# Strip-ordered keys, ready-made bias tables and split stack loads in an encoder layer on one core

## The chip, the cores and the metric

The kernel runs on one core of a Trainium2 chip. The metric is device time in microseconds (us). The kernel before took 1975.67 us, the median of 3 runs (1966.2 to 1977.8).

## The reference

One layer of an encoder over 1024 tokens of 1024 features, in float32. A half-weighted SwiGLU feed-forward block, then attention, then a second feed-forward block; each with an RMS norm before and after it.

```python
h = swiglu(rmsnorm(x, ffn1_pre_g[l]), ffn1_w_gate[l], ffn1_w_up[l], ffn1_w_down[l])
x = x + 0.5 * rmsnorm(h, ffn1_post_g[l])
h = rmsnorm(x, mix_pre_g[l])
qkv = (h @ w_qkv[l]).reshape(B, S, 3, N_HEADS, HEAD_DIM).transpose(2, 0, 3, 1, 4)
o_na = neighbourhood_attention(q[:, :N_HEADS_NA], k[:, :N_HEADS_NA], v[:, :N_HEADS_NA], na_rel_bias[l])
o_dil = dilated_mixture_attention(q[:, N_HEADS_NA:], k[:, N_HEADS_NA:], v[:, N_HEADS_NA:], t5_rel_bias)
...
mixed = jnp.concatenate([o_na, o_dil], axis=-1) @ w_out[l]
x = x + rmsnorm(mixed, mix_post_g[l])
h = swiglu(rmsnorm(x, ffn2_pre_g[l]), ffn2_w_gate[l], ffn2_w_up[l], ffn2_w_down[l])
x = x + 0.5 * rmsnorm(h, ffn2_post_g[l])
```

There are 16 heads of 64 features. The eight **neighbourhood** heads see the tokens as a grid of 16 rows by 64 columns: a query attends to 8 rows and 16 columns around it, with a learned bias for each row and column offset, and columns outside its window are masked. The eight **dilated** heads mix attention over three windows (128 neighbours, every fourth token of 512, every sixteenth of 2048), with a bias from 32 buckets of distance; the windows are merged by the denominators of their softmax. The kernel makes the first window in one part and the other two in a second one, in which the tokens are ordered by their residue modulo 4.

## The kernel before

**Stages.** The first feed-forward block, the value projection, the projection to queries and keys (`PairGemm` with the sink `QKPairs`), the four pairs of dilated heads (`DilPair`, pairs 4 to 7), the four pairs of neighbourhood heads (`na_head`, pairs 0 to 3), the output projection and the second feed-forward block follow each other. Each product of large matrices is made from a high and a low part of its operands, in three matrix products (lines 251, 252 and 253).

**Queries and keys.** `QKPairs.put` splits each half of a pair's queries or keys into high and low parts and writes them to DRAM (`c.qk`). The neighbourhood heads cut the grid into eight strips of 8 columns by 16 rows, so 128 tokens. Their queries are written strip by strip; their keys are written in token order, and the score product picks a strip's keys from 16 rows.

**The stack.** For each head `load_stack` brings a tile `st` of 128 partitions by 3 rows of 1024: its upper 64 partitions hold the high part of the queries, the lower 64 the low part; rows 1 and 2 hold the high and the low part of the keys, in both halves. So two matmuls make a score block. Four DMAs load it, all issued by POOL, two for each half of the partitions. The destination has another type (fp32r) than the source. `st` is `q`'s source for the dilated heads: POOL makes a residue-ordered copy of the queries (line 836, `CAST q<-st`), and of the bias table `g` (line 836, `COPY g<-g`).

**A neighbourhood head** takes its strips one by one: two matmuls `sp<-st` (line 1035) give the scores of 128 queries against 2 or 3 strips of keys, DVE adds the bias and takes the maximum (`sb<-sp,nb`, line 847), ACT takes the exponential (line 848), PE transposes the result (`ptp`, line 857), DVE or ACT copies it out of PSUM (`pt`, line 859), and PE multiplies it by the values (`po<-vs,pt`, line 1051). `Ctx.unit` sets PE's order: a strip's scores, then the transposes of the strip three back, then the fillers, then the value product of the strip four back.

**The bias table** `nb` of a head holds 384 columns per query in two forms: as it is for the two strips at the edges, and with the column mask added for the six inner ones. `na_bias` loads the first form from DRAM (`c.nb`) on SP's queue; POOL adds the mask for the second (line 1465, in `next_ready`, called ahead of each head's strip 5 for the head after it).

**Regrouping and merge.** The dilated part of a pair leaves its output in `ob` in another order of tokens. When the pair's second head has finished that part, `regroup` moves it to `obn` with 16 DMAs on SP's queue (line 969); `merge` then weighs the two outputs on DVE and POOL (lines 997, 998) and adds them (line 1001).

**Fillers.** In the last heads, while PE has room, it makes the first sums of the output projection. `nat_fillers` puts 32 closures on a list, each with one step of three matmuls (`nat_mm`) into the PSUM bank `accp`; after four steps ACT copies the bank out (`hs`, line 291). `Ctx.unit` takes them off at an even rate, about one for each strip.

**What sets the order.** PE's order is the program's. A scheduler sets the order of DVE, ACT and POOL's and SP's work from the dependences and from `c.behind`, which holds a step until a named engine's latest instruction has been issued. `c.todo` is a list of small steps that `c.tick` takes one by one. SP and POOL each issue DMAs in their queue's order; an instruction that waits holds all that stands behind it on its engine. `load_head` loads two heads ahead: the stack, the values (`na_v`, 16 DMAs for a pair, line 1009, rows `vs<-v`) and the bias (line 1015).

## Time and profile before

| What | Value |
|---|---|
| Median of 3 runs | 1975.67 us (1966.2 to 1977.8) |
| The profiled execution | 1978.24 us |
| Its span | 1976.5 us |
| Busy time of PE | 1879.0 us (95%) |
| Loads of weights into PE (PEld) | 1565.9 us (79%) |
| DVE, ACT, POOL | 67%, 41%, 16% |

In time from the span's start the stages are: first feed-forward block to about 650, values to 850, queries and keys to 949, dilated heads to 1071, neighbourhood heads to 1225, output projection and second feed-forward block to the end. All that is changed lies between 850 and 1225.

A row of the groups of instructions gives the line, engine and operation, then tile written and tiles read with their shape and type, the number of instructions, busy time and mean ns of one, and the idle time ahead of them with what ended it. In a timeline each row is the start, the duration and the instruction; "SPq" is the time that SP took to issue DMAs; in square brackets stands how long the engine had been idle and what released it. The granted clock is the share of full speed at which PE was let run.

### The profile page before, as it was taken

The numbers are of one execution on the slowest core, as the hardware profiler recorded it, in microseconds if no ns is written. First come the engines' busy times: TensorE is split into PE (matmuls) and PEld (weight loads), VectorE is DVE, ScalarE is ACT, GpSimd is POOL, SyncE is SP. The second block draws the span as 40 slices with busy tenths as digits, with TensorE's granted clock in tenths as the row PEclk, the third lists the DMA queues.
The fourth block names the chain that finished last, engine by engine and source line by source line (L and its number), as shares of the span: only waits on it lengthen the run. The fifth ranks groups of instructions, "written<-read, shape, count | busy, mean of one in ns | idle before, by whom it ended". The sixth has DMA issues, their size and how long they took to land.

```text
span 1976.5 us, 25577 instructions
## 1 busy us (share of the span) xinstructions
PE 1879.0 (95%) x9044; PEld 1565.9 (79%) x9044; DVE 1329.6 (67%) x2235; ACT 808.5 (41%) x1463; POOL 324.2 (16%) x520
## 2 busy tenths in 40 slices
PE   5999999999999999999999788998999999999997
PEld 4888888887888878778898687877888888878886
DVE  5778776775656775577676565676788777745567
ACT  4522233333534454133676545454222333335333
POOL 2101111111000123323434220021011111110000
PEclk8999999999999999999999889999999999999999
DMA  6555565555876667768998962375556655466664
GB/s 232 216 171 176 181 230 203 202 192 213 298 250 207 240 239 261 223 203 245 219 186 153 156 136 48 133 272 203 169 177 206 234 215 192 170 232 221 202 222 141
DMA packets 170433, 398.63 MB, mean 202 GB/s; under 512 B 20080, under 2 KB 41504, under 8 KB 170304
## 3 DMA queue, kind: packets, MB, share of 16 engines
q1 hardware_dynamic: 118800, 222.34, 36.2%
q0 software_dynamic: 50640, 172.55, 27.5%
q10 hardware_dynamic: 864, 2.10, 0.3%
q8 instruction: 71, 1.16, 0.2%
q14 instruction: 58, 0.48, 0.1%
HBM read 272.55 MB, written 127.26 MB: 202 GB/s over the span
## 4 chain that ended last, share of the span: by engine, by line
PE 82%; DMA 7%; DVE 6%; ACT 2%; issue 2%; SPq 1%; POOL 0%; DVEq 0%; POOLq 0%; ACTq 0%
PE mmp L253 17%; PE mmp L252 17%; PE mmp L251 17%; PE accp L252 8%; PE accp L251 8%; PE accp L253 8%; PE trp L159 2%; DMA st<-qk 1%; PE po L1051 1%; PE ptp L857 1%; PE po L951 1%; DMA obn<-ob 1%; DMA praw<-in_wd_dram 1%; PE sp L1035 1%; PE sp L931 1%
## 5 line engine op out<-in xcount | busy, mean ns | idle before, releaser
L251 PE MATMUL mmp<-x,whi 128*128 128x512 f32 (+1 forms) x1464 | 581.0, 397 | 7.5 <-ACT whi L344 3.5
L253 PE MATMUL mmp<-x,wlo 128*128 128x512 f32 (+1 forms) x1464 | 576.7, 394 | 0.7 <-DVE wlo L345 0.6
L252 PE MATMUL mmp<-x,whi 128*128 128x512 f32 (+1 forms) x1464 | 576.1, 394 | 0.5 <-DVE x L161 0.2
L251 PEld LDWEIGHTS mmp<-x,whi 128*128 128x128 f32 x1464 | 278.9, 191 | 67.4 <-ACT whi L344 4.2
L253 PEld LDWEIGHTS mmp<-x,wlo 128*128 128x128 f32 x1464 | 278.7, 190 | 62.4 <-DVE wlo L345 1.9
L252 PEld LDWEIGHTS mmp<-x,whi 128*128 128x128 f32 x1464 | 279.2, 191 | 60.2 <-DVE x L161 1.4
L601 DVE TENSOR_TENSOR pw<-praw,pw 128x1024 fp32r<-128x1024 f32 (+1 forms) x182 | 198.9, 1139 | 127.5 <-ACT pw L600 127.4
L600 ACT CAST pw<-praw 128x1024 fp32r<-128x1024 f32 (+1 forms) x182 | 168.6, 985 | 216.7 <-PE accp L253 168.1
L252 PE MATMUL accp<-pw 128*128 128x512 f32 x616 | 241.5, 392 | 4.9 <-DVE pw L601 4.9
L251 PE MATMUL accp<-pw 128*128 128x512 f32 x616 | 241.8, 393 | 2.5 <-ACT pw L600 2.5
L253 PE MATMUL accp<-pw 128*128 128x512 f32 x616 | 240.9, 391 | 0.0
L344 ACT CAST whi<-wraw 128x1024 fp32r<-128x1024 f32 x129 | 135.3, 1051 | 251.8 <-PE mmp L252 224.1
L345 DVE TENSOR_TENSOR wlo<-wraw,whi 128x1024 fp32r<-128x1024 f32 x129 | 157.7, 1224 | 24.6 <-ACT whi L344 24.5
L252 PEld LDWEIGHTS accp<-pw 128*128 128x128 f32 x616 | 116.3, 189 | 30.4 <-DVE pw L601 6.4
L251 PEld LDWEIGHTS accp<-pw 128*128 128x128 f32 x616 | 116.3, 189 | 27.2 <-ACT pw L600 3.3
L253 PEld LDWEIGHTS accp<-pw 128*128 128x128 f32 x616 | 116.4, 189 | 24.3
L549 POOL DMA_DIRECT2D g<-sg x44 | 23.9, 542 | 473.0 <-DVE sg L542 285.6
L505 DVE TENSOR_TENSOR c<-mmp,u 128x512 f32<-128x512 f32 x52 | 35.9, 691 | 83.5 <-PE mmp L253 83.3
L363 ACT COPY s<-mmp 128x512 f32<-128x512 f32 x52 | 30.5, 587 | 149.4 <-PE mmp L253 147.7
L161 DVE TENSOR_TENSOR x<-trp,x 128x512 fp32r<-128x512 f32 x84 | 57.3, 687 | 36.1 <-ACT x L160 36.0
L344 ACT CAST whi<-traw 128x512 fp32r<-128x512 f32 x52 | 32.4, 622 | 117.3 <-DVE traw L433 58.5
L432 DVE TENSOR_TENSOR wraw<-wraw 128x1024 f32<-128x1024 f32 x52 | 63.6, 1224 | 22.0 <-DMA wraw<-in_wqk_dram 12.6
(223 smaller groups left out, 2767.1 us busy)
## 6 DMA issues: line engine op xcount, KB each, us to landing
praw<-g SPq DMA_DIRECT2D x70, 512.0 KB
wraw<-in_wg_dram SPq DMA_DIRECT2D x44, 512.0 KB
wraw<-in_wu_dram SPq DMA_DIRECT2D x44, 512.0 KB
tr<-in_wd_dram SPq DMA_DIRECT2D x44, 512.0 KB
g<-sg POOLq DMA_DIRECT2D x88, 256.0 KB, 3.7
ts<-tr POOLq DMA_DIRECT2D x22, 1024.0 KB, 4.7
praw<-ts SPq DMA_DIRECT2D x88, 256.0 KB
praw<-in_wd_dram SPq DMA_DIRECT2D x66, 256.0 KB
```

The source lines that it names most:

```text
L159: nc.tensor.transpose(ps[:, j, :], x[:, j * P:(j + 1) * P], c.ident)
L161: nc.vector.tensor_sub(lo, ps, hi.bitcast(F32))
L251: nc.tensor.matmul(out, ahi, bhi, start=start, stop=False, skip_group_check=go_on)
L252: nc.tensor.matmul(out, ahi, blo, start=False, stop=False, skip_group_check=go_on)
L253: nc.tensor.matmul(out, alo, bhi, start=False, stop=stop, skip_group_check=go_on)
L344: nc.scalar.copy(hi, raw)
L345: nc.vector.tensor_sub(lo, raw, hi.bitcast(F32))
L363: self.c.nc.scalar.copy(s, ps)
L432: nc.vector.tensor_sub(r[:, 0:2], r[:, 1:3], r[:, 0:2])
L505: nc.vector.tensor_add(c21, d, u2)
L600: nc.scalar.copy(w[:, side, 0, :m], raw[:, :m])
L601: nc.vector.tensor_sub(w[:, side, 1, :m], raw[:, :m], w[:, side, 0, :m].bitcast(F32))
```

## The change

It has five parts.

1. The keys of the neighbourhood heads are stored by strips, within each of the two halves of the token rows (`p (s r c)`, the halves one after the other), where they were stored in token order. The score product reads them so, and its columns come out strip by strip; the softmax works on contiguous rows.
2. `mask_bias` makes the bias tables of all eight neighbourhood heads during the query and key product: SP loads a table, POOL copies it in the new order of columns and adds the mask for the second form, and POOL's queue writes both to DRAM (`c.nm`). `na_bias` then loads 384 KB in one DMA, and POOL's additions (line 1465) are gone from the heads.
3. The stack's lower half of partitions is loaded by SP's queue, the upper one by POOL's as before; the destination is taken as plain float32.
4. A filler is two steps of three matmuls where it was one, 16 closures instead of 32; `c.rate` follows their number, so that about every second strip has one.
5. `regroup` is called for each quad of blocks (8 DMAs each) instead of once for both. `na_v` loads a pair's values in 8 DMAs of 16 partitions instead of 16 of 8.

The order of PE's and of DVE's work stays but for the fillers. What moves stands on POOL and SP. The first place is POOL in the dilated stage, from the residue-ordered copies to the next pair's stack (`qk_0_83`, `qk_1_84` are the queries and keys of the pair 6, `qk_0_85`, `qk_1_86` those of 7). Before:

```order
L836 COPY q<-st 128x1024
L836 COPY g<-g 128x384
L998 TENSOR_TENSOR oa<-oa,w 128x1024
L997 TENSOR_TENSOR obn<-obn,w 128x8x128
L829 DMA st<-qk_0_83 64x1024
L830 DMA st<-qk_1_84 64x2x1024
L829 DMA st<-qk_0_83 64x1024
L830 DMA st<-qk_1_84 64x2x1024
L836 COPY q<-st 128x1024
```

With the change:

```order
L855 COPY q<-st 128x1024
L1018 TENSOR_TENSOR oa<-oa,w 128x1024
L1017 TENSOR_TENSOR obn<-obn,w 128x8x128
L848 DMA st<-qk_0_83 64x1024
L855 COPY g<-g 128x384
L849 DMA st<-qk_1_84 64x2x1024
L855 COPY q<-st 128x1024
```

The merge's two products stand ahead of the copy of the table, and half of the stack's issues are gone. The second place is SP where the dilated stage ends, from the first value loads of the neighbourhood heads on (`v_87`; `qk_0_71`, `qk_1_72` are the queries and keys of pair 0, `qk_0_73`, `qk_1_74` those of pair 1). Before:

```order
L1009 DMA vs<-v_87 8x8x128 x17
L1015 DMA nb<-nb 128x384
L969 DMA obn<-ob 32x2x132 x16
L1015 DMA nb<-nb 128x384
L1009 DMA vs<-v_87 8x8x128 x15
L1015 DMA nb<-nb 128x384 x2
```

With the change:

```order
L848 DMA st<-qk_0_71 64x1024
L849 DMA st<-qk_1_72 64x2x1024
L1029 DMA vs<-v_87 16x8x128 x8
L1035 DMA nb<-nm 128x768
L989 DMA obn<-ob 32x2x132 x16
L848 DMA st<-qk_0_71 64x1024
L849 DMA st<-qk_1_72 64x2x1024
L1035 DMA nb<-nm 128x768
L848 DMA st<-qk_0_73 64x1024
L849 DMA st<-qk_1_74 64x2x1024
L1029 DMA vs<-v_87 16x8x128 x8
```

The 16 regrouping DMAs are still together, and behind them now stands half of the second head's stack, ahead of its bias table. The third place is POOL at the same point of the program. Before:

```order
L829 DMA st<-qk_0_71 64x1024
L830 DMA st<-qk_1_72 64x2x1024
L1465 TENSOR_TENSOR nb<-nb,cmask 128x384 x2
L829 DMA st<-qk_0_73 64x1024
L830 DMA st<-qk_1_74 64x2x1024
```

With the change:

```order
L848 DMA st<-qk_0_71 64x1024
L849 DMA st<-qk_1_72 64x2x1024
L848 DMA st<-qk_0_73 64x1024
L849 DMA st<-qk_1_74 64x2x1024
L1018 TENSOR_TENSOR oa<-oa,w 128x1024
L1017 TENSOR_TENSOR obn<-obn,w 128x8x128
```

The two additions are gone, so the next stack's issues stand right behind the second head's.

The diff, without the parts that only rename:

```diff
...
-            for k in range(4):
+            for k in (0, 2):
                 def filler(g=g, t=t, k=k, ws=ws, acc=acc):
                     ws.extend(() if ws else nat_weights(c))
                     acc.extend(() if acc else [nat_bank(c)])
-                    nat_mm(c, acc[0], x, t, k, ws, True, True)
-                    if k == 3:
+                    for i in (k, k + 1):
+                        nat_mm(c, acc[0], x, t, i, ws, True, True)
+                    if k:
                         c.nc.scalar.copy(part[:, t, g * T:(g + 1) * T], acc[0])
...
+def mask_bias(c, pool, cm, i):
+
+    nc = c.nc
+    t = pool.tile([P, 384], F32, tag="t", name="nt")
+    nc.sync.dma_start(t, c.nb[i].rearrange("p r e -> p (r e)"))
+    o = pool.tile([P, 2, 384], F32, tag="o", name="no")
+
+    def rows(x):
+        return x.rearrange("p (r d c) -> p d r c", r=16, d=3)
+    to = [o[:, j].rearrange("p (d r c) -> p d r c", r=16, d=3) for j in range(2)]
+    nc.gpsimd.tensor_copy(to[0], rows(t))
+    nc.gpsimd.tensor_add(to[1], rows(t), rows(cm))
+    nc.gpsimd.dma_start(c.nm[i], o)
...
+        elif kind:
+            x = x.rearrange("p (r s c) -> p s r c", r=8, s=8)
+            parts = [e[:, j].rearrange("p (s r c) -> p s r c", r=8, s=8) for j in range(2)]
...
-    for u in range(2):
-        dst = slice(u * 64, u * 64 + 64)
-        nc.gpsimd.dma_start(st[dst, 0, :], q[u, rows, :])
-        nc.gpsimd.dma_start(st[dst, 1:3, :], k[:, rows, :].rearrange("j p n -> p j n"))
+    for u, queue in enumerate((nc.gpsimd, nc.sync)):
+        to = st[u * 64:u * 64 + 64].bitcast(F32)
+        queue.dma_start(to[:, 0, :], q[u, rows, :])
+        queue.dma_start(to[:, 1:3, :], k[:, rows, :].rearrange("j p n -> p j n"))
...
-        if (hd, part, quad) == (1, 1, 1):
-            self.regroup()
+        if hd and part:
+            self.regroup(quad)
...
-        for ci in range(4):
+        for ci in (2 * quad, 2 * quad + 1):
             for b in range(4):
                 nc.sync.dma_start(self.obn[ci:P:4, b:8:4, :], self.ob[32 * b:32 * b + 32, 2 * ci:2 * ci + 2, :])
...
-    src = c.v[0][:, p * P:(p + 1) * P].rearrange("(r s c) f -> r c s f", r=16, s=8)
-    for r in range(16):
-        c.nc.sync.dma_start(vs[r * 8:r * 8 + 8], src[r])
+    src = c.v[0][:, p * P:(p + 1) * P].rearrange("(r s c) f -> c r s f", r=16, s=8)
+    for ci in range(8):
+        c.nc.sync.dma_start(vs[ci:P:8], src[ci])
...
-    c.nc.sync.dma_start(nb[:, 0], c.nb[2 * p + hd].rearrange("p r e -> p (r e)"))
+    c.nc.sync.dma_start(nb, c.nm[2 * p + hd])
...
-        pv = ps[:, :n * P].rearrange("p (r e) -> p r e", r=16)
+        pv = ps[:, :n * P].rearrange("p (d h x) -> p h d x", d=n, h=2)
         for i in range(2):
-            nc.tensor.matmul(pv, lhs, kv[i][:, :, k0 * 8:k1 * 8], start=i == 0, stop=i == 1)
+            nc.tensor.matmul(pv, lhs, kv[i][:, :, k0:k1], start=i == 0, stop=i == 1)
...
+            at = {i: [lambda i=i: mask_bias(c, mk, cm, i)] for i in range(8)}
+            at[5] += [lambda: queued(load_head)]
+            at[7] += [lambda: queued(load_head), lambda: queued(first_bias)]
+            plan(8, at)
...
-                    else:
-                        nc.gpsimd.tensor_add(g[:, 1], g[:, 0], c.cmask)
```

More of the change, by code (lines that the diff above doesn't have):

```diff
@@ L793, in put @@
         e = c.sp.tile([P, 2, T], F32R, tag="qk", name="qk", bufs=c.qkbufs)
-        strip = kind == 0 and p < NP
+        strip = p < NP
         parts = [e[:, 0], e[:, 1]]
@@ L810, in put @@
         for j in range(2):
-            if strip:
+            if strip and kind == 0:
                 dst = d[j].rearrange("p (s r c) -> p s (r c)", s=8, r=16)[:, :, h * 64:h * 64 + 64]
@@ L961, in outs, with regroup @@
             c.todo.extend([lambda: None] * 3 + [lambda: c.behind(self.merge, DVE, ACT)])
-    def regroup(self):
+    def regroup(self, quad):
         c, nc = self.c, self.c.nc
-        self.obn = c.op.tile([P, 8, RW], F32, tag="obn", name="obn")
-        for ci in range(4):
+        if quad == 0:
+            self.obn = c.op.tile([P, 8, RW], F32, tag="obn", name="obn")
+        for ci in (2 * quad, 2 * quad + 1):
             for b in range(4):
@@ L1020, in na_head @@
     nc = c.nc
-    kv = [st[:, 1 + i].rearrange("p (r w) -> p r w", r=16) for i in range(2)]
+    kv = [st[:, 1 + i].rearrange("p (h s x) -> p h s x", h=2, s=8) for i in range(2)]
     for s in range(8):
@@ L1132, in layer @@
         c.v = [c.dr.tile([SEQ, 512], F32, name=f"v{g}") for g in range(2)]
-        c.ob = [c.dr.tile([SEQ, RW], F32, name=f"ob{g}") for g in range(4)]
+        c.nm = c.dr.tile([8, P, 2, 384], F32, name="nm")
         x1 = [c.dr.tile([P, D], F32, name=f"x1_{t}") for t in range(8)]
@@ L1415, in layer @@
         nc.sync.dma_start(gd[:, 512:D], a["dil_out_g"].broadcast_to([P, 512]))
-        c.cmask = c.at.tile([P, 384], F32, tag="cmask", name="cmask", bufs=1)
-        nc.sync.dma_start(c.cmask, a["cmask"])
         xo = {}
```

14 lines of the change are left out of this document (6 added, 8 removed).

## The prediction

> **What bounds the kernel now.** The page's first part says that TensorE (PE) sets the end; the question is where it doesn't run at its pace. The table of stretches (columns: stretch, its length, busy time of PE, PEld, DVE, ACT, POOL, granted clock, DMA share, GB/s) splits the span by stage: query/key GEMM, dilated heads, neighbourhood heads before and with the fillers.
>
> ```profile
> PE 1879.0 (95%) x9044; PEld 1565.9 (79%) x9044; DVE 1329.6 (67%) x2235; ACT 808.5 (41%) x1463; POOL 324.2 (16%) x520
> ```
> ```profile
> 850.00:949.00 99.00, 97.29 (x423) 80.31 (x424) 72.37 (x94) 37.22 (x48) 31.91 (x49) 0.98 0.75 216
> 949.00:1071.00 122.00, 113.79 (x978) 111.88 (x977) 81.97 (x334) 92.14 (x305) 52.96 (x57) 0.99 0.99 189
> 1071.00:1160.00 89.00, 68.07 (x428) 62.08 (x428) 52.19 (x166) 44.79 (x141) 21.04 (x29) 0.83 0.89 153
> 1160.00:1225.00 65.00, 61.56 (x413) 55.21 (x413) 32.88 (x104) 37.77 (x106) 6.52 (x10) 1.00 0.47 85
> ```
>
> All that the change touches lies in 850 to 1225. The GEMM is PE-bound. The dilated stage is nearly PE-bound and its DMA engines are full (0.99). From 1071 to 1160 PE idles 21 us and the rest runs at clock 0.83: there is time to win. What ended PE's idle time from 1071 to 1225 (total, times, longest):
>
> ```profile
> PE sp L1035 <- DMA st<-qk: 5.5, 1, 5.5
> PE ptp L857 <- DVE pt L859: 4.5, 2, 3.0
> PE po L1051 <- DVE pt L859: 4.0, 2, 3.1
> PE accp L251 <- ACT hs L291: 3.4, 4, 1.0
> PE po L1051 <- ACT pt L859: 3.3, 2, 3.0
> PE sp L1035 <- DVE stt L847: 2.3, 3, 1.3
> ```
>
> **The change part by part.** Heads below are neighbourhood heads 1 to 8. The sum is made against the profiled execution, 1978.24 us with a span of 1976.5; it is 2.6 us above the median of 1975.67.
>
> Term A, the third head's stack. These are the timelines of SP, POOL, DVE and PE around the last regrouping:
>
> ```profile
> 1056.12 15.09 SPq L1009 DMA_DIRECT2D vs<-v  x17
> ...
> 1071.97 15.12 SPq L969 DMA_DIRECT2D obn<-ob  x16
> 1087.20 0.53 SPq L1015 DMA_DIRECT2D nb<-nb  x1
> ...
> 1076.12 1.00 POOL L1465 TENSOR_TENSOR nb<-nb,cmask 128x384 f32<-128x384 f32 x1 [2.80 <-DMA nb<-nb]
> 1090.15 1.00 POOL L1465 TENSOR_TENSOR nb<-nb,cmask 128x384 f32<-128x384 f32 x1 [13.02 <-DMA nb<-nb]
> 1091.09 0.55 POOL L829 DMA_DIRECT2D st<-qk  x1
> ...
> 1090.06 0.42 DVE L847 CUSTOM_DVE_ANT_1 sb<-sp,nb 128x256 f32<-128x256 f32 x1 [3.60 <-DMA nb<-nb]
> ...
> 1085.75 0.49 PE L1035 MATMUL sp<-st 128*128 128x256 f32 x2
> 1092.27 1.65 PE L1051 MATMUL po<-vs,pt 128*128 128x128 f32 x6 [3.11 <-DVE pt L859]
> 1097.80 0.60 PE L1035 MATMUL sp<-st 128*128 128x384 f32 x2
> 1099.15 0.49 PE L1035 MATMUL sp<-st 128*128 128x256 f32 x2
> 1106.16 0.76 PE L1035 MATMUL sp<-st 128*128 128x256 f32 x2 [5.53 <-DMA st<-qk]
> 1108.50 0.99 PE L1035 MATMUL sp<-st 128*128 128x384 f32 x2
> 1111.06 0.67 PE L1035 MATMUL sp<-st 128*128 128x384 f32 x1
> ```
>
> Read upwards: head 3 starts at 1106.16 because its stack was issued only at 1091.09, on POOL behind the mask addition of head 2's bias, which had stood 13.02 us waiting for a load that SP issued at 1087.20, behind 16 regrouping DMAs. Head 3's buffer was free when head 2 began, 1085.75. The change makes the tables ahead, so POOL doesn't wait there: its half goes out some 5 us earlier, SP's half behind head 2's bias. The 5.53 goes. So does the cold clock after it: two strips took 4.90 us (1106.16 to 1111.06) where one takes 1.35 (1097.80 to 1099.15), so 2.2 lost. A = -7.7, from -5.5 (cold all the same) to -7.7.
>
> Term B, the second head's bias and stack. The gap of 3.11 at 1092.27 ends a DVE wait of 3.60 for that bias. On SP it stays behind the regrouping, and head 2's stack half now stands there too. But SP carries 8 value loads where 16 stood, so the regrouping can start before 1071.97, as its first half is written, and half of the stack that crowded it comes later. Best: nothing is late, -3.6 (3.11, and 0.5 of cold clock). Worst: the half issues at 1087.2 and, landing 1 us later than the bias did, costs +1. I take -2.5. Calling the regrouping twice moves no DMA in the queue.
>
> Term C, fillers. The accumulator has one bank, so each group of fillers waits for the copy of the one before: 3.4 us in four waits. With two products' worth in a filler and every second strip without one, the copy has a strip's time. Also the first product behind the transposes is longer (columns: busy, mean ns):
>
> ```profile
> L251 PE MATMUL accp<-whi,o 128*128 128x512 f32 x34 | 16.3, 478 | 3.4 <-ACT hs L291 3.4
> L252 PE MATMUL accp<-wlo,o 128*128 128x512 f32 x34 | 13.3, 392 | 0.0
> ```
>
> 16 such places fewer at 0.086 is 1.4. C = -4, from -4.8 to 0.
>
> Term D, POOL against DVE. POOL's additions lengthen DVE's work on the norms:
>
> ```profile
> 1140.56 1.80 DVE L143 TENSOR_TENSOR e<-e,y 128x4 f32<-128x4 f32 x1
> 1142.79 0.16 DVE L143 TENSOR_TENSOR e<-e,y 128x4 f32<-128x4 f32 x1
> 1143.47 0.86 DVE L144 SCALAR_TENSOR_TENSOR y<-e,y 128x4 f32<-128x4 f32 x1
> ...
> 1147.63 0.69 PE L857 MATMUL ptp<-ident,pb 128*128 128x128 f32 x2 [3.01 <-DVE pt L859]
> ...
> 1140.00:1160.00 20.00, 15.32 (x80) 13.63 (x79) 15.27 (x34) 8.48 (x20) 3.32 (x5) 0.66 0.82 177
> ```
>
> Against the 0.16 of the row between (the 0.86 likewise), DVE lost 2.3 us just ahead of PE's gap of 3.01, and then the clock stays low. The additions go, half of the issues stay. If the gap shrinks to 0.7 and the clock stays up, 2.3 and up to 4.7 are won (0.34 of 20 us is 6.8, less what other gaps cost). I take -3, from -7 to 0. The Trainium skill (TensorE: Matmul & The Clock Gate, Part 1) puts the window of the gate at about 3.4 us, free-running; by that rule a gap of 0.7 would not cool the array. The trace agrees in part: it is cold behind a gap of 3.01 as well.
>
> Term E, the dilated stage. Two edits pull against each other. POOL's products of the merge now stand ahead of the copy that waits for a bias table, which frees this:
>
> ```profile
> 1046.04 1.23 DVE L1001 TENSOR_TENSOR og<-oa,obn 128x1024 f32<-128x1024 f32 x1 [2.13 <-POOL obn L997]
> 1048.61 1.16 PE L951 MATMUL po<-va,pt 128*128 128x128 f32 x8 [2.46 <-DVE pt L859]
> ```
>
> That is -2.5. But SP's half of the stack for each pair's second head stands behind that regrouping:
>
> ```profile
> 1007.65 11.21 SPq L969 DMA_DIRECT2D obn<-ob  x16
> 1025.17 0.72 PE L931 MATMUL sp<-st,q 128*128 128x256 f32 x4
> ...
> L836 POOL CAST q<-st 128x1024 fp32r<-128x1024 f32 x7 | 14.6, 2092 | 44.9 <-DMA st<-qk 40.5 <-PE sp L931 4.5
> st<-qk POOLq DMA_DIRECT2D x16, 512.0 KB, 9.0
> ```
>
> The regrouping ends at 1018.9; two issues at some 0.7 each (11.21 for 16), a landing between 4.5 (half the bytes on the queue) and 9.0, and the cast of 2.1 by which the residue-ordered queries are made give 1026 to 1030.5, where PE wants them at 1025.17: 1 to 5 us late, and behind the waiting cast stand the next table's copy and the next stack's POOL half. Three pairs: +3 to +15. E runs from -2.5 to +12.5; as loads in this stage land slowly only when it is crowded, and half of each has left POOL's queue, I take +3.
>
> Term F, the GEMM: eight times a POOL copy and an addition (1.00 above), a load, and a store that POOL issues. POOL was busy 31.9 of 99 us; 16 more fit, and the DMA share of 0.75 has room for 4.7 MB (21 us at 216 GB/s would be all of it, so it is nearly full). Weights are loaded a pair ahead. 0, to +5 where a weight load stands behind a bias load waiting for POOL. The strip order of the keys adds nothing there: the same copies with other strides.
>
> Term G: of the 2.3 us for which scores waited for DVE, some 1.0 is head 1's, whose DVE work waits for POOL's addition at 1076.12 (the longest, 1.3, stands at 1153): -1, from -1.1 to 0. Term H: bias tables of twice the bytes, 0.2 MB more, 1 us a head at 189 GB/s, for the three heads before DMA has air: +1, from 0 to +3. The softmax on contiguous rows: 0, the same elements.
>
> Sum: -7.7 - 2.5 - 4 - 3 + 3 + 0 - 1 + 1 = -14.2, so 1964.0 for such an execution and, 2.6 us less, about **1961 us** for the median.
>
> **The rivals.** First, two rings fill both partition halves at once. A stack's halves follow each other on one queue now, and it moves slowly (first row: almost a stack alone; second: weights and a bias table over 128 partitions):
>
> ```profile
> 1164.00:1172.00 8.00, 8.00 (x58) 7.37 (x57) 4.48 (x14) 5.01 (x13) 0.34 (x1) 1.00 1.29 204
> 1183.00:1186.00 3.00, 3.00 (x22) 2.71 (x21) 1.16 (x5) 1.56 (x4) 2.03 (x4) 1.00 1.10 332
> ```
>
> A stack is 1.5 MB (on each half of the partitions 256 KB of queries and 512 KB of keys). At 332 instead of 204 GB/s (last column) it lands in 4.7 instead of 7.7 us, the late halves in E vanish, and A to D and G come at their best: -7.7 - 3.6 - 4.8 - 7 - 2.5 - 1.1 + 1 = -25.7, so 1952.5, median 1950. Against it: the dilated stage has a DMA share of 0.99 with all sixteen engines. The Trainium skill (SBUF — State Buffer, "Can I just issue two DMAs to hit both halves?") says no: two at once measured only 6% more than one. By it a stack would take 7.3 us, and this rival falls; no run here shows it yet.
>
> Second, slower: SP's order holds up the second heads. The place is the stack half behind L969; if it lands more than about 10 us behind the last regrouping issue, each pair loses 5 us, and the array cools behind such a gap (2.2 as in A): 7.2 four times, with B's head, is +29, F adds 5, H 3; A and C give 12 back: about +25, 2003, median 2000. For it: 15.12 us for 16 DMAs where loads crowd. Against it: the late half is half.
>
> Third, nothing moves: what was waited for at 1092 and 1106 is waited for at the next burst of DVE and ACT work, which the change doesn't touch; A falls to -3, D to 0, C stays at -2, E at +3: 1976, median 1974.
>
> **How the numbers follow.** Forecast 0.45 (its own range 1951 to 1971), the first rival 0.27, the second 0.15, the third 0.13. One per cent, about what a measurement of this kernel can tell from no change, is 19.8 us: faster below 1955.9, slower above 1995.4. Faster: 0.27 and 0.13 of the forecast, 0.40. Slower: 0.15. Within: 0.45. The range, 1944 to 1990, leaves about 0.1 out above and less below.
>
> **What would show it.** Right: no wait of POOL for nb, no gap of 5 us ahead of head 3, no accp wait on hs, clock near 1 from 1085 to 1115. E: gaps at L931 on st or q. The first rival: stretches with a stack alone above 300 GB/s. Wrong: the stretch 1071 to 1160 as long as before, or the dilated stage more than 10 us longer.

## The result, and the profile after

The changed kernel took 1978.32 us (median of 20 executions, 1972.67 to 1989.94), the kernel before, on the same chips, 1972.97 us (20 executions, 1966.2 to 1978.68). The ratio is 1.003, 95% interval 1.0018 to 1.0043. Faster by about 14.7 us was forecast; it is slower by some 5.

One execution of e1 below, 2120.51 us at a clock of 0.841, is left out of its ratio.

The profiled execution of the changed kernel took 1983.87 us, with a span of 1982.1 against 1976.5; both profiled executions lie some 5 us above their medians. PE's busy time is that of before (1876.8 us against 1879.0). The table of stretches, cut here where each kernel's own stages begin and end (columns as in the prediction; the first three rows are of the kernel before, the last three of the changed one), shows two large shifts that nearly cancel:

```profile
835.97:948.75 112.78, 110.80 (x482) 91.13 (x481) 77.75 (x100) 39.32 (x50) 37.62 (x60) 0.98 0.75 223
948.75:1071.18 122.43, 114.22 (x982) 112.31 (x980) 82.21 (x334) 92.32 (x307) 53.39 (x58) 0.99 0.99 189
1071.18:1244.38 173.20, 144.75 (x911) 129.13 (x910) 97.40 (x305) 90.12 (x271) 29.55 (x42) 0.90 0.65 118
```
```profile
834.10:967.96 133.86, 116.82 (x482) 94.47 (x481) 82.31 (x100) 38.74 (x50) 58.33 (x86) 0.92 0.75 238
967.96:1098.05 130.09, 118.38 (x982) 116.36 (x980) 81.61 (x334) 92.17 (x307) 41.88 (x39) 0.95 0.76 167
1098.05:1249.79 151.74, 133.14 (x912) 120.32 (x910) 94.77 (x305) 91.05 (x271) 13.61 (x20) 0.97 0.58 141
```

The query and key GEMM (first row of each, from its first product on `mmp` to the first dilated score, 482 matmuls in both) is 21.1 us longer, with the clock at 0.92 instead of 0.98. The dilated stage is 7.7 longer. The stretch from the first neighbourhood score to a fixed point in the output projection is 21.5 shorter. The GEMM began 1.9 us earlier than before. Together that makes +5.4 of the 5.6 us between the spans. Of what ended PE's idle time in the changed kernel from 850 to 1240 (total, times, longest), these rows matter here:

```profile
PE mmp L251 <- DVE v L479: 15.1, 4, 9.3
PE sp L950 <- DMA st<-qk: 5.0, 3, 3.6
PE ptp L876 <- DVE pt L878: 3.4, 2, 2.0
PE sp L1055 <- DMA st<-qk: 3.0, 1, 3.0
```

The first row did not exist before. The wait of 5.5 ahead of the third head and those for `hs` are gone, as forecast; there are new waits for stacks in the dilated stage (L950, 5.0) and at the second neighbourhood head (L1055, 3.0).

Now the first gap of 9.3, followed upwards. These are timelines of the changed kernel: DVE, SP, POOL, then DVE and PE.

```profile
869.36 1.22 DVE L346 TENSOR_TENSOR wlo<-wraw,whi 128x1024 fp32r<-128x1024 f32 x1
...
877.82 0.32 SPq L775 DMA_DIRECT2D nt<-nb  x1
878.19 0.55 SPq L339 DMA_DIRECT2D wraw<-in_wqk_dram  x1
...
876.33 0.50 POOL L781 COPY no<-nt 128x384 f32<-128x384 f32 x1 [2.92 <-DMA nm<-no]
876.79 1.00 POOL L782 TENSOR_TENSOR no<-nt,cmask 128x384 f32<-128x384 f32 x1
...
886.68 1.23 DVE L433 TENSOR_TENSOR wraw<-wraw 128x1024 f32<-128x1024 f32 x1 [11.05 <-DMA wraw<-in_wqk_dram]
...
896.82 0.77 PE L251 MATMUL mmp<-x,whi 128*128 128x512 f32 x1 [9.26 <-DVE v L479]
```

The weights' buffer was free at 870.6, when DVE had split the ones before. SP issued the next load only at 878.19, behind a table load at 877.82, which waited for the table's single tile. POOL gave that tile back at 877.79, with the end of an addition whose copy had itself waited 2.92 us for the store of the table before. DVE took the weights up at 886.68, and PE stood until 896.82. In the kernel before, the same two places read:

```profile
885.75 0.56 SPq L338 DMA_DIRECT2D wraw<-in_wqk_dram  x1
...
892.25 1.23 DVE L432 TENSOR_TENSOR wraw<-wraw 128x1024 f32<-128x1024 f32 x1 [1.09 <-DMA wraw<-in_wqk_dram]
```

Before, DVE already waited 0.7 to 1.1 us for its weights in each of five turns (4.7 us in all). DVE had no slack to spend; PE had a little, as e8 will show.

### The profile page after: what moved, and what is told of

It reads as the page before. It is cut to its first block, busy times and chain, and to the rows that moved or that the text cites. A ratio compares the mean times of both kernels' runs of the same rounds, so it can differ in the third digit from the quotient of the medians.

```text
span 1982.1 us, 25603 instructions
## 1 busy us (share of the span) xinstructions
PE 1876.8 (95%) x9044; PEld 1564.1 (79%) x9044; DVE 1331.1 (67%) x2235; ACT 808.0 (41%) x1463; POOL 316.4 (16%) x504
## 4 chain that ended last, share of the span: by engine, by line
PE 77%; DMA 8%; DVE 7%; issue 3%; ACT 2%; POOL 1%; SPq 0%; DVEq 0%; ACTq 0%; POOLq 0%
PE mmp L253 15%; PE mmp L251 15%; PE mmp L252 15%; PE accp L252 8%; PE accp L253 8%; PE accp L251 8%; PE po L970 2%; DMA wraw<-in_wqk_dram 2%; PE trp L159 1%; PE ptp L876 1%; PE po L1067 1%; PE sp L950 1%; DMA praw<-in_wd_dram 1%; DVE wlo L346 1%; DMA st<-qk 1%
## 5 line engine op out<-in xcount | busy, mean ns | idle before, releaser
L251 PE MATMUL mmp<-x,whi 128*128 128x512 f32 (+1 forms) x1464 | 583.6, 399 | 22.5 <-DVE v L479 15.1
L602 DVE TENSOR_TENSOR pw<-praw,pw 128x1024 fp32r<-128x1024 f32 (+1 forms) x182 | 199.1, 1139 | 129.1 <-ACT pw L601 128.9
L346 DVE TENSOR_TENSOR wlo<-wraw,whi 128x1024 fp32r<-128x1024 f32 x129 | 159.6, 1240 | 22.8 <-ACT whi L345 22.8
L253 PEld LDWEIGHTS accp<-pw 128*128 128x128 f32 x616 | 116.0, 188 | 24.2
```

The lines of the kernel that those rows point to most:

```text
L251: nc.tensor.matmul(out, ahi, bhi, start=start, stop=False, skip_group_check=go_on)
L253: nc.tensor.matmul(out, alo, bhi, start=False, stop=stop, skip_group_check=go_on)
L346: nc.vector.tensor_sub(lo, raw, hi.bitcast(F32))
L602: nc.vector.tensor_sub(w[:, side, 1, :m], raw[:, :m], w[:, side, 0, :m].bitcast(F32))
```

## The experiments

All ratios are to the kernel before on the same chip, with 95% intervals. A ratio is made from all executions and can differ a little from the quotient of two medians. Stage lengths are those of one profiled execution each, cut as above: GEMM, dilated stage, neighbourhood heads (with the fixed point as their end). Such a length varies by some microseconds: in e7, e11 and e17, whose totals moved by 0.12% at most, the heads last 167.7, 168.5 and 169.4 us against 173.2 before, so 4 to 5 of the 21.5 us may belong to the one execution that was profiled before.

### Why the GEMM got longer

**e1: the heads' loads ahead of the table.** `queued` ties a step to the latest work of SP and POOL, so behind a table load the dilated heads' loads had moved ahead of weights.

```diff
-            at[5] += [lambda: queued(load_head)]
-            at[7] += [lambda: queued(load_head), lambda: queued(first_bias)]
+            at[5].insert(0, lambda: queued(load_head))
+            at[7][:0] = [lambda: queued(load_head), lambda: queued(first_bias)]
```

> The loads of the first two dilated heads are asked for ahead of the bias table of the same turn instead of behind it, so they no longer follow the table's load on SP; all else is the changed kernel. In its trace the query and key GEMM ends 19.2 us later than before, with PE waits of 9.3 (behind a weight load that SP issued 7.6 us after its buffer was free, behind a table load) and 4.3 (behind a weight load that took 12.9 us among the heads' loads). Queue theory (weights come late because of what stands ahead of them on SP): the 4.3 and its cold clock go, the 9.3 stays: about 1971 us. Traffic theory (the tables' 4.7 MB slow each weight load wherever they stand): the loss stays, 1976 to 1978.

Measured: 1978.04 us, 1.0032 (1.0013 to 1.0051): nothing won. PE's gaps at the same place are spread, not smaller:

```profile
PE mmp L251 <- DVE v L479: 14.6, 5, 5.9
```

So the heads' loads were not the second cause; the queue theory's number for this run was wrong.

**e2: the tables loaded on POOL's queue.**

```diff
-    nc.sync.dma_start(t, c.nb[i].rearrange("p r e -> p (r e)"))
+    nc.gpsimd.dma_start(t, c.nb[i].rearrange("p r e -> p (r e)"))
```

> mask_bias loads its tables on POOL's queue, where its stores stand already; the bytes are the same, SP carries no table. Queue theory: every weight load is issued as soon as its buffer is free, the PE waits of 9.3 and 4.3 go, the stage is as long as before: 1978 - 17 = about 1961 us. Traffic theory: weights still land 2 to 6 us late, the stage stays some 12 us longer than before: about 1973 us or more.

Measured: 1976.85 us, 1.0029 (1.0011 to 1.0047). The queue theory, as it stood, fell: SP issues every weight load at once, and the stage is as long as in the changed kernel. The waits of ACT, of POOL (both from 850 to 970) and of PE say where the time went:

```profile
ACT qk L826 <- DMA qk<-qk: 29.4, 5, 12.7
POOL no L781 <- DMA nt<-nb: 42.4, 7, 10.4
PE mmp L251 <- DVE v L479: 16.8, 4, 7.5
```

POOL's copy now waits for a load in its own queue, 42.4 us in all. Behind the copy stand the stores of queries and keys, which POOL issues too. Until they are done the `qk` buffers are not free, ACT waits to cast into them (29.4 us; before, not at all; in the changed kernel once, 13.4 us), and behind that cast stand its splits of the weights. The chain was moved from SP to POOL, and it held up something else. Left were two explanations: the chain's waits, or its 4.7 MB of traffic.

**e8: the traffic without the waits.** It leaves the biases out of its result, and POOL's copies and additions with them.

```diff
-    t = pool.tile([P, 384], F32, tag="t", name="nt")
+    t = pool.tile([P, 384], F32, tag="t", name="nt", bufs=2)
     nc.sync.dma_start(t, c.nb[i].rearrange("p r e -> p (r e)"))
...
-    nc.gpsimd.tensor_copy(to[0], rows(t))
-    nc.gpsimd.tensor_add(to[1], rows(t), rows(cm))
     nc.gpsimd.dma_start(c.nm[i], o)
...
-            at = {i: [lambda i=i: mask_bias(c, mk, cm, i)] for i in range(8)}
+            at = {i: [lambda i=i: queued(lambda: mask_bias(c, mk, no, i))] for i in range(8)}
```

> The changed kernel, in which the query and key GEMM carries the tables' traffic but none of their waits: each turn SP loads a table that nobody reads (two buffers) and POOL stores 384 KB out of one tile that was made once from the mask, so the biases are left out of the result; the loads of the dilated heads are asked for ahead of it as in e1. Bytes: the same 4.7 MB. Wait theory (POOL's chain of load, copy and store in queues that work in order holds up the weight loads on SP and the stores of queries and keys on POOL, so their buffers, so ACT and DVE): the stage is as long as before, about 1978 - 17 = 1961 us. Traffic theory: it stays 12 us or more longer, 1973 us or more.

Measured: 1964.11 us, 0.9964 (0.9947 to 0.9982). The GEMM's row, what is left of PE's wait there, and DVE's wait for weights:

```profile
835.23:949.10 113.87, 111.09 (x482) 91.04 (x481) 77.52 (x100) 39.23 (x50) 40.24 (x65) 0.99 0.81 264
```
```profile
PE mmp L251 <- DVE v L479: 0.8, 1, 0.8
DVE wraw L433 <- DMA wraw<-in_wqk_dram: 8.9, 5, 3.5
```

With all bytes of the tables (264 GB/s against 223 before) the stage lasts 113.9 us, 1.1 more than before. DVE waits 8.9 us for weights instead of 4.7, and PE loses 0.8 by it. The traffic theory fell. Left are the waits and POOL's own work, which this run leaves out; e12 has both the bytes and the work.

**e12: the chain a turn apart, stacks on POOL alone.** Each turn POOL works on the table that SP loaded a turn earlier.

```diff
+            def table(i):
+                if i:
+                    mask_bias(c, mk, cm, i - 1, nts.popleft())
+                if i < 8:
+                    nts.append(mask_load(c, mk, i))
-            at = {i: [lambda i=i: mask_bias(c, mk, cm, i)] for i in range(8)}
+            at = {i: [lambda i=i: queued(lambda: table(i))] for i in range(8)}
...
-    for u, queue in enumerate((nc.gpsimd, nc.sync)):
+    for u, queue in enumerate((nc.gpsimd, nc.gpsimd)):
```

> All five parts, mended in two places: both halves of the stack on POOL's queue, and the tables' chain drawn apart: SP loads a table one turn of the GEMM ahead of POOL's copy and addition (two buffers), each tied to the latest work of both queues, and the dilated heads' loads are asked for ahead of it. The work and the bytes in the GEMM are those of the changed kernel. Wait theory: the GEMM lasts as before plus 0 to 3 us, the dilated stage 122 to 125, the heads 148 to 150: 1953 to 1957 us. Traffic theory, or POOL's own work (8 copies and additions beside DVE): the GEMM stays over 10 us longer: 1965 us or more.

Measured: 1972.82 us, 1.0009 (0.9997 to 1.0021). With real tables the GEMM takes 116.5 us (first row), 3.8 more than before in place of 21.1: so the waits were the main cost. The edit brings a second buffer, a turn's distance, a tie to both queues and the heads' loads ahead, and does not divide these. The forecast of the time was wrong all the same: the dilated stage lasts 128.1 us (122 to 125 expected) and the heads 160.0 (148 to 150). The largest gap is at the second neighbourhood head (SP, DVE and PE).

```profile
830.91:947.44 116.53, 111.85 (x482) 90.90 (x480) 82.38 (x100) 39.55 (x50) 53.14 (x80) 0.99 0.78 246
```
```profile
1075.03 14.35 SPq L994 DMA_DIRECT2D obn<-ob  x16
1089.54 0.47 SPq L1040 DMA_DIRECT2D nb<-nm  x1
...
1099.07 0.42 DVE L871 CUSTOM_DVE_ANT_0 sb<-sp,nb 128x256 f32<-128x256 f32 x1 [10.63 <-DMA nb<-nm]
...
1100.57 1.65 PE L1072 MATMUL po<-vs,pt 128*128 128x128 f32 x6 [9.44 <-DVE pt L883]
```

Its table of 384 KB is issued behind 16 regrouping DMAs and lands 9.5 us later, so PE stands 9.4 us.

**e13: the changed kernel with the chain a turn apart, nothing else.** The same edit as in e12, the stacks still split.

> The changed kernel with one thing else: the tables' chain is drawn apart over two turns of the GEMM and the dilated heads' loads are asked for ahead of it, as in e12; the stacks stay split over two queues. Wait theory: the GEMM ends as before (e12: 112.4 us in the window that was 132.9), the dilated stage and the heads stay as in the changed kernel (130 and 152): 1978 - 17 = about 1961 us, range 1958 to 1965. Rival (the loss only moves on to the heads, as e12's 1973 might mean): 1970 us or more.

Measured: 1965.85 us, 0.997 (0.9953 to 0.9988); the changed kernel stood at 1.003. The three stages:

```profile
833.57:949.55 115.98, 110.24 (x482) 89.70 (x481) 81.92 (x100) 39.27 (x50) 52.22 (x78) 1.00 0.80 257
949.55:1077.18 127.63, 116.82 (x981) 113.75 (x980) 83.28 (x334) 92.06 (x307) 47.84 (x48) 0.97 0.85 187
1077.18:1227.17 149.99, 130.58 (x911) 117.59 (x910) 94.82 (x305) 91.22 (x271) 13.61 (x20) 0.99 0.60 143
```

The GEMM's loss is down to 3.2 us (116.0 us against 133.9, 112.8 before) and did not move on to the heads. By the medians 12 of the 17 us that were expected came back, just outside the range given. Those 3.2 are part of the missing 5; the profiled execution is the shortest of its 12 (1958.8 to 1970.5 us), and the rest stays open.

**e14: e12 with the bias loads on POOL's queue.**

```diff
+            nb = na_bias(c, p, hd) if p < NP else None
             st = load_stack(c, p, hd)
...
-    c.nc.sync.dma_start(nb, c.nm[2 * p + hd])
+    c.nc.gpsimd.dma_start(nb, c.nm[2 * p + hd])
```

> As e12 (tables made ahead a turn apart, stacks on POOL alone), but the neighbourhood heads' bias tables, of 384 KB, are loaded on POOL's queue ahead of the last three DMAs of their stack, so not behind the regrouping. Place theory: the gap of 9.4 us ahead of the second head's first value product goes with its cold clock, 10 to 11 us: about 1962 us. Size theory (the bytes in front of it are late wherever they stand): the stack comes later instead, 1968 to 1973 us.

Measured: 1967.05 us, 0.9977 (0.9959 to 0.9995), 5.8 below e12, between the two theories. The gap at the second head shrinks from 9.4 to 4.1:

```profile
PE po L1072 <- DVE pt L883: 4.7, 2, 4.1
```

Place and size both seem to count; the run does not divide them further, and its profiled execution, too, is the shortest of its 12 (1959.7 to 1976.2 us).

### Where the gain at the heads came from

**e3 and e4: the parts in two groups.** e3 is the kernel before with parts 3, 4 and 5 (stack halves, fillers, regrouping and value loads). e4 is the kernel before with parts 1 and 2 (strips and tables).

> Parts 1 and 2 are undone (keys in token order, POOL adds the mask at the heads); stack halves on two queues, longer fillers, regrouping in two halves and value loads stay. Both theories: the GEMM is as long as before. What it shows is how much of the attention's gain of 14 us belongs to these three parts: if the ready-made tables bring most of it (terms A, D and G of the prediction, some 12 of 21), the neighbourhood heads gain only about 8 and the dilated stage loses its 7: about 1972 us. Rival: the second queue brings most of it (a stack lands sooner on two): about 1962 us.

> Only parts 1 and 2: strip-ordered keys and tables made ahead; stacks on POOL alone, short fillers, one regrouping, 16 value loads. The GEMM loses its 15 to 19 us in both theories. If the tables bring most of the gain at the heads (12 of 21) and the dilated stage keeps its length: 1973 + 17 - 12 = about 1978 us. Rival (the second queue brings it): 1973 + 17 - 3 = about 1987 us.

Measured: e3 1962.19 us, 0.9953 (0.9936 to 0.997); e4 1990.5 us, 1.0098 (1.0074 to 1.0123). The numbers are near the rival's in both (1962 and 1987), by luck: its reason, the second queue, falls with e7 below. e3's dilated stage and heads:

```profile
946.27:1073.85 127.58, 117.19 (x981) 114.82 (x980) 81.34 (x334) 92.30 (x307) 44.02 (x42) 0.96 0.79 176
1073.85:1227.04 153.19, 134.12 (x912) 121.58 (x911) 95.10 (x305) 91.18 (x271) 22.32 (x28) 0.96 0.56 131
```

Without the ready-made tables the heads last 153.2 us, with them 151.7 (the changed kernel): on top of the other parts the tables bring 1.5 of the 21.5 us, and cost 21 in the GEMM. Alone they bring more: e4's heads last 162.7, 10.5 less than before. POOL issues the third stack there without any wait for a bias table, as soon as PE has freed the buffer, and PE's wait of 5.5 ahead of the third head is gone. Against that stands a gap of 9.4 ahead of the second head's first value product, as in e12, which also gives that stack more time (POOL, then PE, of e4):

```profile
1110.55 0.51 POOL L847 DMA_DIRECT2D st<-qk  x1 [14.62 <-PE sp L1053]
```
```profile
PE po L1065 <- DVE pt L877: 9.7, 2, 9.4
```

**e5, e6 and e7: the second queue.** In e5 only the neighbourhood heads' stacks are split. In e6 both halves are on POOL, still as plain float32. e7 is the kernel before with the split alone.

```diff
-    for u, queue in enumerate((nc.gpsimd, nc.sync)):
+    for u, queue in enumerate((nc.gpsimd, nc.sync if p < NP else nc.gpsimd)):   # e5
+    for u, queue in enumerate((nc.gpsimd, nc.gpsimd)):                          # e6
```

> As e3 (no tables ahead), but only the neighbourhood heads' stacks are split over two queues; the dilated heads' stay on POOL. In e3 the dilated stage lasted 127.6 us against 122.4 before, with PE waiting 5.7 us for a stack. If SP's halves behind the regrouping are the cause: the stage goes back to 122 to 123, the neighbourhood heads stay as in e3: about 1957 us. Rival (the regrouping in two halves or the order on POOL is the cause): 1962 us as e3.

> As e3, but both halves of every stack on POOL's queue, still into a tile taken as plain float32; so against e3 only the second queue goes. If the second queue brings the gain of the neighbourhood heads (153 us against 173): they go back by 8 or more, the dilated stage gains 5: about 1966 us. If the plain type, the fillers, the value loads and the regrouping bring it: heads as in e3, the dilated stage 5 shorter: about 1957 us.

> The kernel before with the stack halves on two queues alone (short fillers, 16 value loads, one regrouping, no tables ahead). Second-queue theory: of the 20 us that the neighbourhood heads gained in e3 some 12 to 15 come from it, the dilated stage loses 5: 1971.4 - 8 = about 1963 us. Rival (fillers, value loads and regrouping bring most): 1971.4 - 5 + 5 = about 1971 us.

Measured: e5 1959.77 us, 0.9944 (0.9924 to 0.9964); e6 **1954.76 us**, 0.9915 (0.9893 to 0.9937); e7 1971.39 us, 1.0002 (0.9986 to 1.0018). The dilated stage and the heads, of e5, of e6 and of e7:

```profile
945.37:1070.18 124.81, 115.63 (x982) 113.58 (x980) 82.31 (x334) 92.19 (x307) 52.21 (x56) 0.97 0.85 189
1070.18:1225.42 155.24, 135.15 (x911) 121.97 (x910) 95.64 (x305) 91.03 (x271) 22.02 (x28) 0.96 0.55 128
```
```profile
948.14:1072.93 124.79, 117.01 (x982) 115.12 (x980) 82.56 (x334) 92.38 (x307) 49.35 (x55) 0.96 0.85 189
1072.93:1222.79 149.86, 132.29 (x912) 119.14 (x911) 95.15 (x305) 90.79 (x271) 35.38 (x44) 0.98 0.56 132
```
```profile
947.81:1076.13 128.32, 116.47 (x981) 113.94 (x980) 83.66 (x334) 92.24 (x307) 43.95 (x42) 0.97 0.79 175
1076.13:1243.79 167.66, 137.87 (x911) 123.11 (x910) 96.69 (x305) 90.03 (x271) 21.80 (x28) 0.94 0.50 120
```

e6 came out a little below the number for a second queue that brings nothing (1957), e7 at its rival's (1971), e5 between its two. The second queue gains nothing and costs: against e6 the split takes 5.0 us at the neighbourhood heads (e5; the two intervals just overlap, the executions, 1954.9 to 1964.9 us against 1948.0 to 1956.6, hardly) and 7.4 with the dilated ones (e3). Where the dilated heads' stacks are split, PE waits 5.7 (e3) and 4.6 us (e7) for them in that stage, where they are not, 0.7 (e5) or not at all (e6): SP's half stands behind the regrouping, as the prediction's term E had it. The stage's length alone is a weaker sign: 127.6 and 128.3 us with the split against 124.8 twice without it, but 128.1 and 129.1 in e12 and e14, which have no second queue either. Half a stack still lands slowly when both queues carry one. Rows of the DMAs of 1075 to 1230, of the kernel before and of the changed one (KB of each, median us from issue to landing):

```profile
st<-qk POOLq DMA_DIRECT2D x12, 512.0 KB, 9.8
```
```profile
st<-qk SPq DMA_DIRECT2D x8, 512.0 KB, 7.2
st<-qk POOLq DMA_DIRECT2D x8, 512.0 KB, 9.5
```

**e9, e10 and e11: the other edits one by one**, each alone on the kernel before: the longer fillers, part 5, and the plain type with both halves on POOL.

> The kernel before with the longer fillers alone. The neighbourhood heads of the kernel with parts 3, 4 and 5 and no second queue (e6) last 149.9 us against 173.2. The prediction's term C: 3.4 us of PE's waits for the copy go, and 1.4 of longer first products: 4 us less, about 1967 us. If the rate of the fillers does more (PE's work in the last heads lies otherwise beside DVE's): 10 us less, 1961. If the waits only move: 1971.

> The kernel before with part 5 alone: 8 value loads for a pair instead of 16, regrouping by quads. Theory: SP is 8 issues or some 8 us a pair shorter, so the biases that stand behind the value loads and the regrouping come sooner, POOL's addition waits less and the next stack, which POOL issues behind it, comes sooner: the wait of 5.5 ahead of the third head goes with its cold clock: 5 to 8 us less, about 1965 us. Rival (the plain type of the stack brings it): 1970 to 1972 us.

> The kernel before with the stack taken as plain float32 alone, both halves still on POOL's queue. In e6 a stack's DMA of 512 KB landed 7.9 us after its issue in the neighbourhood heads (median), before 9.8; of 256 KB 5.8 against 7.8. Theory: the loads that convert are the slower ones, each stack lands some 2 us sooner and the queue is free sooner: 5 to 10 us less, 1962 to 1967 us. Rival (e7 with it and the second queue gained nothing, so the type does nothing): 1970 to 1972 us.

Measured: e9 1967.58 us, 0.9979 (0.9964 to 0.9995); e10 1958.55 us, 0.9938 (0.9917 to 0.9958); e11 1970.4 us, 0.9988 (0.9977 to 0.9999). On 1972 us that is -4.1, -12.2 and -2.4, each within some 2 to 4 us, together -18.7; e6, which has all three, has -16.8. The expectation for e9 (1967 us) held, that for e10 was short by 6. For the type its rival held: the median landing of 512 KB with it was 9.9 us, with the conversion 9.8.

**e16 and e17: the two edits of part 5**, apart.

```diff
-    src = c.v[0][:, p * P:(p + 1) * P].rearrange("(r s c) f -> r c s f", r=16, s=8)
-    for r in range(16):
-        c.nc.sync.dma_start(vs[r * 8:r * 8 + 8], src[r])
+    src = c.v[0][:, p * P:(p + 1) * P].rearrange("(r s c) f -> c r s f", r=16, s=8)
+    for ci in range(8):
+        c.nc.sync.dma_start(vs[ci:P:8], src[ci])
```

> The kernel before with the value loads of a pair in 8 DMAs of 16 partitions in place of 16 of 8, and nothing else. Value theory: the second pair's value loads, which stood with a DMA share of 0.5 to 0.6 and 60 to 100 GB/s ahead of the third head's stack, are shorter and go earlier, the regrouping starts sooner: nearly all of e10's 12 us: about 1960 us. Rival (the regrouping does it): 1968 to 1971 us.

> The kernel before with the regrouping called by quads, 8 DMAs each, and nothing else. The prediction's own statement: no DMA moves in the queue, no change, 1970 to 1972 us. Rival: the first half is issued while the second quad still computes and the second heads' biases come sooner: 1960 to 1966 us.

Measured: e16 1959.55 us, 0.9944 (0.9925 to 0.9963); e17 1972.44 us, 1.0005 (0.9989 to 1.002). The value loads do it all, to within these intervals. In e16 the heads last 152.6 us, at a clock of 0.98; POOL and PE at the third head:

```profile
1070.36:1222.98 152.62, 132.80 (x911) 119.00 (x910) 95.09 (x305) 90.04 (x271) 33.28 (x44) 0.98 0.64 129
```
```profile
1086.13 1.00 POOL L1465 TENSOR_TENSOR nb<-nb,cmask 128x384 f32<-128x384 f32 x1 [9.74 <-DMA vs<-v]
1087.08 0.55 POOL L829 DMA_DIRECT2D st<-qk  x1
...
1096.91 0.48 PE L1035 MATMUL sp<-st 128*128 128x256 f32 x2 [1.61 <-DMA st<-qk]
```

POOL's addition still waits 9.74 us ahead of the stack's issue. From the heads' start the third stack is issued 16.7 us on (before: 19.9), and PE begins 9.8 us after the issue (before: 15.1). So 3.2 of the 8.4 us are an earlier issue and 5.3 a quicker landing. Before, the second pair's value loads ran ahead of that stack. The DMA view of the kernel before from 1089.5 to 1092, when almost nothing but these loads was moving:

```profile
DMA packets 493, 0.22 MB, mean 90 GB/s; under 512 B 56, under 2 KB 493, under 8 KB 493
...
q1 hardware_dynamic: 493, 0.22, 53.9%
```

During these loads of 8 partitions about half of the sixteen DMA engines' time was used, at 90 GB/s. The Trainium skill (DMA: Bandwidth & Descriptors, "Why a DMA increments its semaphore by 16 and not by 1") says that a DMA is spread over the largest number of engines, at most 16, that divides the slowest dimension of both sides: 8 for 8 partitions, 16 for 16. The 53.9% is near the half that this gives for 8. But SP issued 15 of these loads of 32 KB in 5.42 us (1087.77 to 1093.19), which also makes some 90 GB/s, so the pace of the issues could have set the rate as well. No stretch of e16 shows the new loads alone, so their own rate stays open, and so does how much of the gain is the rate and how much the smaller number of issues.

**e15: the best version.** e6 with the small bias loaded on POOL's queue, the same edit as e14's.

> As e6 (no tables ahead, stacks on POOL alone, plain type, longer fillers, part 5), with the bias tables, of 192 KB, on POOL's queue ahead of the last three DMAs of their stack. In e6 the second and third heads still waited 1.9 and 1.6 us for their stacks, which POOL issued behind additions that waited 12.0 and 9.5 us. Place theory: these waits shrink, 2 to 4 us less than e6's 1954.8, 1951 to 1953 us. Rival: POOL's queue gets 192 KB more ahead of the stack and the stack comes later: 1955 to 1959 us.

Measured: **1952.22 us**, 0.9903 (0.9882 to 0.9923). PE's wait for stacks at the heads, of e6 and of e15:

```profile
PE sp L1037 <- DMA st<-qk: 3.4, 2, 1.9
```
```profile
PE sp L1037 <- DMA st<-qk: 1.3, 2, 0.7
```

The waits shrink as the place theory said, but the ratios of e6 and e15 overlap: which of the two is faster isn't settled. Both are faster than the kernel before and than the changed one, with the longer fillers, the plain type, the value loads and the halved regrouping, without the tables ahead and without the second queue.

## Why the prediction was wrong, step by step

- **Term F is the step that failed, by its size.** It put the tables' chain at 0, at most 5; the GEMM became 21.1 us longer. Its upper bound named the right wait, a weight load behind a bias load that waits for POOL. But the value came from POOL's busy time and the bytes ("16 more fit"), which contain no waiting, and from "Weights are loaded a pair ahead", which the trace of before contradicts: the load issued at 885.75 is the one that DVE takes up at 892.25, after a wait of 1.09 us. The two sums as such were nearly right: the bytes cost 1.1 us (e8), bytes and POOL's work together 3.2 to 3.8 (e12, e13). The other 17 or so were waiting: a chain of load, copy and store with one buffer each, in two queues that work in order. In the changed kernel it held weight loads up on SP and once the stores of queries and keys on POOL, in e2 these stores. A row from before pointed at it: DVE waited for its weights in each of five turns.
- **A (-7.7)**: the wait of 5.5 went, and POOL's wait for the bias with it; but the tables were not the only cure. Alone they let the third stack out without that wait (e4). The new value loads alone have the gain too, with POOL's wait of 9.74 still in place (e16), mostly by a quicker landing. The prediction followed the third stack up to its late issue and stopped there; it did not ask why that stack then took 15 us, where the median of its kind was 9.8. The value loads stood in the text only as a reason why the regrouping could start sooner. On top of them the tables bring 1.5 us (e3); as the two gains overlap, the changed kernel's 21.5 cannot be divided between them.
- **B (-2.5)** came to about nothing: the wait of 3.11 for the bias went, and PE waits 3.0 us for the second head's stack instead (L1055), whose half on SP is issued only at 1107.97, behind the 16 regrouping DMAs. B named that place and priced it at +1 at worst. The sentence that regrouping by halves moves nothing held (e17).
- **C (-4)** held: -4.1 (e9, between -7.1 and -1.0), and the waits for `hs` are gone there.
- **D (-3)** is not shown: the gap ahead of the transposes went from 3.0 to 2.0 with the additions gone, but in e16, with all additions in place, it is 2.2 and the clock at the heads 0.98. What they cost lies within the 1.5 us of e3 against the changed kernel.
- **E (+3, from -2.5 to +12.5)**: 7.7 in the profile, inside its bounds. PE's waits for stacks grew from 0.4 to 5.0, by the mechanism named (e3 and e7 against e5 and e6). The rest is not assigned: e9, whose edit does not touch this stage, has 124.6 us against 122.4. The term's own numbers add up to 1026.9 to 1031.4, so 1.7 to 6.2 us late for each pair, not 1 to 5.
- **G (-1)**: that kind of wait fell from 2.3 to 0.8 us, a little beyond its bound; but in e16, without the tables, it is gone as well. **H (+1)** was too small where the stack is on POOL alone: a table of twice the size behind the regrouping cost the second head 9.4 us (e12, e4).
- **The signs** that the prediction named for being right nearly all came (no gap of 5 ahead of the third head, no wait for `hs`, a clock of 0.97 at the heads instead of 0.90), and neither sign of being wrong did. None of them looked at the GEMM.
- **The rivals.** The first (two queues fill a stack at once) fell: the split alone gives 1.0002. The Trainium skill (SBUF — State Buffer, "Can I just issue two DMAs to hit both halves?") says that two DMAs at once, one to each half, measured only 6% over a single one. That agrees with e7, which shows the kernel's time and not the rate. The second (SP's order holds up the second heads) has its mechanism in the 5.0 us of L950 and the 3.0 of L1055, some 8 of the 29 us that it was priced at; the kernel is slower, but mainly for another reason. In the third, nothing was to move; much moved and cancelled.

For the heads the sum of A, B, C, D, G and H was -17.2, the profile has -21.5, by luck in part, since A, B and D did not come as described. With E and F at their measured sizes the sum would have been 1989.8 for the profiled execution's 1983.87; the difference is 4.3 at the heads and 1.9 ahead of the GEMM. One stage was closed with a sum over resources where a chain of waits decided.

## What to carry to other kernels

Ahead of putting a chain of load, compute and store into a stage that runs at its bound, look for the transfer that is waited for a little in every turn: what stands ahead of it in its queue, waiting, can hold it up for long, even if bytes and engine time have room. Loading a turn ahead, into a second buffer and tied to both queues' work, brought the same chain's cost from 21.1 us down to 3.2 here (e13). Of a buffer that comes late, ask both when it was issued and how long it then took, and what shared the DMA engines with it. And measure the parts of a bundle alone: here three gained some 4, 12 and 2 us, the second queue cost 5 to 7, and the tables made the changed kernel 16 us slower than e3. Two edits that remove the same wait do not add up.

## What the runs showed of the hardware that was not expected

While transfers over 8 partitions ran nearly alone, 53.9% of the DMA engines' time was used and 90 GB/s moved; moving the same bytes in half as many transfers, of 16 partitions each, took 0.56% off the whole kernel (e16, between 0.37% and 0.75%). A second queue for half of a stack gave no gain (1.0002). After the gap of 9.26 us PE's matmuls took 0.63 us instead of 0.39 until 902.07; in these 5.3 us they started 0.43 us apart instead of 0.23, so about 2.5 us of lower clock came on top of the gap.
